# Six convolution taps on ScalarE and the DMA engines, two block sums by DMA, and one store on another queue

## The chip, the cores and the metric

The kernel runs on one core of a Trainium2 chip. A core has five instruction streams that run beside each other and wait for each other by semaphores: TensorE (PE in the profile; PEld is its weight load), VectorE (DVE), ScalarE (ACT), GpSimd (POOL) and SyncE (SP), which here only issues transfers. Transfers are issued from the queues of SP, ACT and POOL and carried out by 16 DMA engines that the queues share. A transfer issued from POOL can add what it reads to what stands at its target ("accumulating transfer" below). The metric is the device time of one execution in microseconds, the median of the runs.

## The reference

One block of a streaming encoder, for a sequence of 512 with 1024 channels, in float32:

```python
h = h + 0.5 * _swiglu(_rmsnorm(h, ffn1_norm), ffn1_w_in, ffn1_w_out)      # D_FF = 2816
z = _rmsnorm(h, mix_norm) @ w_in
conv_a, conv_gt, q, k, v, r, g_lr = split(z)                              # 512, 512, 256, 256, 512, 512, 16
y_conv = _conv_module(conv_a, conv_gt, conv_w, conv_b, conv_ln_g, conv_ln_b)
y_gla  = _gla(q, k, v, r, g_lr, gate_w_up, gate_b, gla_norm)              # 4 heads, chunks of 64
h = h + concatenate([y_conv, y_gla]) @ w_out
h = h + 0.5 * _swiglu(_rmsnorm(h, ffn2_norm), ffn2_w_in, ffn2_w_out)
h = h + sigmoid(_rmsnorm(h, ple_norm) @ ple_w_gate) * (p @ ple_w_proj)
out = _rmsnorm(h, final_norm)

def _conv_module(a, b, w_dw, b_dw, ln_g, ln_b):
    glu = a * sigmoid(b)
    y = causal_depthwise_conv(glu, w_dw, width=31) + b_dw                 # 512 channels, each with its own 31 taps
    return silu(_layernorm(y, ln_g, ln_b))                                # mean and variance over the 512 channels
```

The case is about the convolution (31 taps for each channel) and the LayerNorm behind it, whose mean needs the sum over all 512 channels.

## The kernel before, in words

Channels lie on the 128 partitions and time along a row, so most tiles are 128x512 in float32 (256 KB). Matrix products are made in three matmuls of a reduced-precision type: each weight is split into a high part (`wh`, a cast by ScalarE) and a low part (`wl` = weight - high part). The low part is either a DVE subtraction (`low`) or, with `added`, two steps: ScalarE writes the negated high part to `wl`, and a transfer on GpSimd's queue adds the raw weight to it.

The stages follow one another: the first FFN to about 337 us, the mixer to about 520 us, the second FFN to about 845 us, then the gate of the per-layer input, the last norm and the stores. In the mixer come the input projections (blocks of output channels, `zblock`, then blocks of time, `tokblock`), the chunks of the linear attention, and the output projection, whose first half over the attention channels (`first_part`) runs before the convolution's channels are ready.

The convolution has four blocks of 128 channels, c = 0 to 3, with the sums in `acc[c]` (`cv` in the trace) and the inputs in `glu[c]` (`glr`, `glu`, `glu` and `en` in the trace's rows of taps, since buffers are named by their first tenant). `conv_steps(c)` (line 1013) is a generator: the first step writes the last tap with the bias, the next 30 steps add one tap each, all on DVE. Tap w is late by 30 - w columns, so that the first tap (w = 0) covers 482 columns and the last of them (w = 29) 511. `taps(n)` (line 1025) takes n steps, in turn from the two oldest convolutions that are not done; calls of it stand between the other DVE work of the mixer. What is left of the last one is run through behind `first_part(1, ...)` (line 1456).

For the LayerNorm's mean the four blocks are added to `acc012` (`r` in the trace): two DVE additions at lines 1424 and 1439, between taps, and `acc[3]` at line 1460 behind the last tap. PE multiplies it with the constant matrix `mean`, inside `first_part(5, ...)` at its step 6; DVE then subtracts the mean from each `acc[c]`, ScalarE squares, DVE adds the squares.

The order of PE, DVE and ScalarE is that in which the code is written: the helper class `Ordered` (line 46, which is why nearly all rows of the trace name L46) ties each instruction behind the one before it on its engine. The transfers on SP and GpSimd are ordered by the scheduler of the tile framework. A transfer waits on its issuing queue until its data and its target are ready, and all later ones on that queue wait behind it.

At the prediction's places the names are: `wl<-wr` on POOL, low parts of weights by `added` (wk[1] of the key projection, wo[2] of the output projection); `sm<-wr`, the low part of an early piece of the per-layer input's product; `wa<-wr` x4, the low parts of wo[4] and wo[5] in four tiles of 256 KB; `wr<-in_w_out` and `wr<-in_ffn_w_in` on SP, loads of raw weights. The last four stores of the tail are made by `first_half`, `scaled_out` and `second_half` (lines 1815 to 1831), with the calls from line 1942.

Of the kernel before, what the change touches and what calls it, by code (L numbers as in the profile page):

```python
# [11 lines left out]
AF = mybir.ActivationFunctionType  # L12
ALU = mybir.AluOpType
PSUM = bass.MemoryType.PSUM

P = 128
SEQ = 512
# [4 lines left out]
WIDTH = 31  # L22
PAD = WIDTH - 1
# [39 lines left out]
def block_kernel(ctx: ExitStack, tc: tile.TileContext, a: dict, out: bass.AP):  # L63
    nc = tc.nc
    pe, dve, act, pool = (Ordered(tc, e) for e in (nc.tensor, nc.vector, nc.scalar, nc.gpsimd))
# [15 lines left out]
    def nm(s):  # L81
        uid[0] += 1
        return f"{s}_{uid[0]}"
# [6 lines left out]
    def bt2(dt=F32R, s="a"):  # L90
        t = big.tile([P, 2, SEQ], dt, tag="A", bufs=NA, name=nm(s))
        hi, lo = t[:, 0], t[:, 1]
        whole_of[id(hi)] = hi, t
        return hi, lo

    def bt(dt=F32, s="a"):
        if dt not in other:
            t, other[dt] = bt2(dt, s)
            return t
        return other.pop(dt)  # L100

    def cvt(dt=F32, s="cv"):
        return big.tile([P, SEQ], dt, tag="CV", bufs=NCV, name=nm(s))

    def tmp(s, w=SEQ, dt=F32, bufs=2):
        return tp.tile([P, w], dt, tag=s, bufs=bufs, name=nm(s))
# [65 lines left out]
    cw = col[:, ncol - DC:]  # L172
# [5 lines left out]
    def vec(name, c, n=1):  # L178
        at = first_of[name] + c
        return col0[:, at:at + n] if at < DC else col[:, at - DC:at - DC + n]  # L180
# [42 lines left out]
    def high(r3):  # L223

        nk, nc_ = r3.shape[1], r3.shape[2]
        hi = wp.tile([P, 1024], F32R, tag="wh", bufs=6, name=nm("wh"))
        lo = wp.tile([P, 1024], F32R, tag="wl", bufs=6, name=nm("wl"))
        h3 = hi[:, :nk * nc_].rearrange("p (k c) -> p k c", k=nk)
        l3 = lo[:, :nk * nc_].rearrange("p (k c) -> p k c", k=nk)
        act.copy(h3, r3)  # L230
        return h3, l3, r3
# [6 lines left out]
    def added(w):  # L238

        h3, l3, r3 = w  # L240
        act.mul(l3, r3, -1.0)
        pool.dma_start(out=l3.bitcast(F32), in_=r3, accum_op=ALU.add)
        return w
# [766 lines left out]

    glu, acc, conv = [], [cvt() for _ in range(4)], []

    def conv_steps(c):
        y, g, tap = acc[c], glu[c], cw[:, c * WIDTH:(c + 1) * WIDTH]
        dve.tensor_scalar(y, g, tap[:, PAD:WIDTH], vec("conv_b", c), ALU.mult, ALU.add)
        yield
        for w in range(PAD):
            late = PAD - w
            dve.scalar_tensor_tensor(out=y[:, late:], in0=g[:, 0:SEQ - late], scalar=tap[:, w:w + 1],
                                     in1=y[:, late:], op0=ALU.mult, op1=ALU.add)  # L1020
            yield

    turn = [0]

    def taps(n):

        for _ in range(n):
            if not conv:
                return
            i = turn[0] % min(2, len(conv))  # L1030
            turn[0] += 1
            try:
                next(conv[i])
            except StopIteration:
                conv.pop(i)
# [8 lines left out]
    def glu_value(ps):  # L1044
        a1 = tmp("u1")
        dve.tensor_tensor(out=a1, in0=ps, in1=rsb, op=ALU.mult)
        return a1

    def glu_out(a1, sg):
        g = bt(s="glu")  # L1050
        dve.tensor_tensor(out=g, in0=a1, in1=sg, op=ALU.mult)
        glu.append(g)
        conv.append(conv_steps(len(glu) - 1))
# [50 lines left out]

    taps(1)
    wq.append(added(high(raw_q[1])))


    pb = zblock(w2b[0], hg)
# [44 lines left out]
    wk.append(added(high(raw_k[1])))  # L1154
    taps(5)
    glu_out(glu_value(pa), sg)


    qdec, qneg, kneg, kpos, kdec = [], [], [], [], []
# [49 lines left out]
    def tokblock(w, t, mid={}):  # L1209

        ps = bank()
        ts = slice(t * P, (t + 1) * P)
        i = 0
        for k in range(DC):
            wh, wl = w[k // 2][:2]
            xh, xl = hg[k]
            for x, y in ((xh, wh), (xl, wh), (xh, wl)):
                if i in mid:
                    mid[i]()
                pe.matmul(ps, x[:, ts], y[:, k % 2, :], start=(i == 0), stop=(i == 3 * DC - 1))  # L1220
                i += 1
        return ps
# [31 lines left out]
    def chunk_sums(cs):  # L1254
        for j in range(2):
            if len(kvs) == j:
                kvs.append([bank(), bank()])
            for c in cs:
                s0 = (c % 2) * CH
                for i in range(2):  # L1260
                    h = 2 * j + i
                    pe.matmul(kvs[j][c % 2][i * HK:(i + 1) * HK, (c // 2) * HV:(c // 2 + 1) * HV],
                              kdt[j][s0:s0 + CH, (c // 2) * P + i * HK:(c // 2) * P + (i + 1) * HK],
                              vt[c // 2][s0:s0 + CH, h * HV:(h + 1) * HV], start=True, stop=True)
# [18 lines left out]
    def out_of(t, h):  # L1283
        c = 2 * (t % 2) + h // 2
        return ops[2 * (t // 2) + h % 2][:, c * HV:(c + 1) * HV]
# [21 lines left out]
    def chain(cs):  # L1307
        for c in cs:
            for j in range(2):
                state(j, c)  # L1310
# [39 lines left out]
    def early_parts():  # L1350
        hi, lo = (kept_p[:, i * 2 * P:(i + 1) * 2 * P].rearrange("p (k c) -> p k c", k=2) for i in range(2))
        act.copy(hi, early_p)
        added((hi, lo, early_p))
        early_x[:] = [(hi[:, k], lo[:, k]) for k in range(2)]
        wh, wl = (wp.tile([P, 1024], F32R, tag="sm", bufs=2, name=nm("sm")).rearrange("p (k c) -> p k c", k=2)
                  for _ in range(2))
        act.copy(wh, early_w)
        early_wh[:] = added((wh, wl, early_w))[:2]
# [3 lines left out]
    def oload(n):  # L1362
        for i in range(n, n + 2):
            raw_o[i] = load(a["w_out"], 0, DC, i * P, P)

    def ohigh(n):
        return (high4 if n in (4, 5) else high)(raw_o[n])
# [21 lines left out]
    for t in range(TB):  # L1389
        if t == 0:  # L1390
            ps = tokblock(wr, t, {5: lambda: chunk_sums(range(7))})
            chain(range(7))
            taps(3)
            oload(4)
        elif t == 1:
            ps = tokblock(wr, t, {2: outputs})
            early_parts()
            taps(15)
            by_t = "p (t h) -> p t h"
            so3 = so.rearrange(by_t, h=4)  # L1400
            dve.tensor_tensor(out=so3, in0=so3, in1=rs2.unsqueeze(2).to_broadcast([P, TB, 4]), op=ALU.mult)
            rso = rsqrt_mean(so, HV * HK, 16, between=lambda: taps(5))
            rso3 = rso.rearrange(by_t, h=4)
            dve.scalar_tensor_tensor(out=rso3, in0=rso3, scalar=HK ** -0.5,
                                     in1=rs.unsqueeze(2).to_broadcast([P, TB, 4]), op0=ALU.mult, op1=ALU.mult)
        else:
            ps = tokblock(wr, t)
        r = bt(s="r")
        act.activation(r, ps, AF.Silu, scale=rs[:, t:t + 1])
        rt.append(r)  # L1410
        if t == 1:
            oload(2)
            for n in (4, 5):
                wo[n] = [added(w) for w in ohigh(n)]
            ytok = []
            for i in range(TB):
                y = bt(s="y")
                for h in range(4):
                    vs = slice(h * HV, (h + 1) * HV)
                    act.activation(y[:, vs], out_of(i, h), AF.Copy, scale=rso[:, 4 * i + h:4 * i + h + 1])  # L1420
                ytok.append(y)
        if t == 3:
            acc012 = bt(s="acc012")
            dve.tensor_tensor(out=acc012, in0=acc[0], in1=acc[1], op=ALU.add)
        if t > 0:
            taps((0, 2, 5, 1)[t])
            for i in {1: (0,), 2: (1, 2), 3: (3,)}[t]:
                dve.tensor_tensor(out=ytok[i], in0=ytok[i], in1=rt[i], op=ALU.mult)
# [7 lines left out]
            pe.transpose(yps[h][:, t * P:(t + 1) * P], ytok[t][:, h * HV:(h + 1) * HV], ident)  # L1436
    pe.matmul(pq, early_x[0][0], early_wh[1][:, 0, :], start=False, stop=False)
    projected(pq, 0, early_wh, early_x, (1,))
    dve.tensor_tensor(out=acc012, in0=acc012, in1=acc[2], op=ALU.add)
    taps(1)  # L1440
    for h in range(4):
        mix[4 + h] = gsplit(yps[h], vec("gla_norm", h), "yg")
# [89 lines left out]
    for k in range(4):  # L1532
        for n in range(3):
            w, ps = half[n]
# [199 lines left out]
    hf, hl = {}, {}  # L1734
# [77 lines left out]
        dve.scalar_tensor_tensor(out=q, in0=r, scalar=nh, in1=r, op0=ALU.mult, op1=ALU.mult)  # L1812
        dve.scalar_tensor_tensor(out=q, in0=q, scalar=1.5, in1=r, op0=ALU.add, op1=ALU.mult)

    def scaled_out(t, e, src, *queue):
        y = bt(s="y")
        act.activation(y, src, AF.Copy, scale=roots[t][2])
        put(t, e, y, *queue)

    def put(t, e, y, queue=nc.sync):  # L1820
        queue.dma_start(out=out[0, t * P:(t + 1) * P, e * SEQ:(e + 1) * SEQ], in_=y)

    def first_half(t, e):
        y = bt(s="y")
# [3 lines left out]
    def second_half(t, e):  # L1828
        y = bt(s="y")
        dve.scalar_tensor_tensor(out=y, in0=hl[t], scalar=roots[t][2], in1=gfin[e], op0=ALU.mult, op1=ALU.mult)  # L1830
        put(t, e, y)
# [110 lines left out]
    first_half(0, 0)  # L1942
    scaled_out(0, 1, gained)
    newton(1)
    scaled_out(1, 0, hf[1], act)
    second_half(1, 1)


# [48 lines left out]
```

## Time and profile before

| | |
|---|---|
| time, median of 3 runs (lowest, highest) | 921.93 us (921.61, 922.09) |
| profiled execution, its own time | 921.48 us |
| its span, first to last instruction | 919.7 us |
| mean granted TensorE clock | 0.998 |
| PE busy | 910.7 us (99%) |
| DVE busy | 816.7 us (89%) |
| ACT busy | 511.7 us (56%) |
| POOL busy | 60.3 us (7%) |
| mean DMA rate | 129 GB/s |

The page gives shares of one profiled execution. A share is a mean over all stages: DVE is 89% busy over the whole span and 19.45 of 20 us from 460 to 480 us. A row of a timeline has the start in us, the duration in us, the engine, line, operation, target<-sources, and in brackets the engine's idle time before it with what ended it; x18 means that 18 instructions in a row were put together, with the time from the first start to the last end. Rows with a q behind the engine are issues of transfers; how long these take to land stands in the DMA view (number, KB each, median us from issue to landing).

### The profile page before, as it was taken

What the parts mean: (1) busy time and instruction counts of PE and PEld (TensorE: products, weight loads), DVE (VectorE), ACT (ScalarE), POOL (GpSimd) and SP (SyncE); (2) the same over time, 40 slices, a digit from 0 to 9 for tenths busy, and PEclk for the clock granted to TensorE, in tenths of its full rate; (3) what the DMA queues carried; (4) which work ended last, traced back from release to release, by engine and by line L of the source; (5) the groups of instructions that cost most, each with busy time, mean ns of one, the idle gap of its engine ahead of it and who ended that gap; (6) DMA issues with size and microseconds to landing.
All of it is one profiled execution on the core that took longest, in us unless ns stands there. A gap on an engine that the chain in (4) does not pass through costs nothing.

```text
span 919.7 us, 12838 instructions
## 1 busy us (share of the span) xinstructions
PE 910.7 (99%) x4948; PEld 779.7 (85%) x4948; DVE 816.7 (89%) x1090; ACT 511.7 (56%) x746; POOL 60.3 (7%) x76
## 2 busy tenths in 40 slices
PE   9999999999999999999999999999999999999996
PEld 8899888888888887788887889888888888888885
DVE  6699989999989766999996779899999999997896
ACT  7755354445454574463665875455445444556884
POOL 0120000000000111001130020000000000000121
PEclk9999999999999999999999999999999999999999
DMA  9534333224334692245572563333223322358454
GB/s 350 186 100 136 117 112 122 91 73 135 115 92 115 158 295 51 69 118 158 139 166 93 137 157 97 115 116 126 87 84 130 122 89 87 118 155 240 92 99 131
DMA packets 37149, 118.89 MB, mean 129 GB/s; under 512 B 4192, under 2 KB 4960, under 8 KB 37088
## 3 DMA queue, kind: packets, MB, share of 16 engines
q1 hardware_dynamic: 30176, 97.22, 31.8%
q0 software_dynamic: 6624, 20.58, 12.5%
q8 instruction: 39, 0.64, 0.3%
q10 hardware_dynamic: 288, 0.27, 0.1%
q14 instruction: 22, 0.18, 0.1%
HBM read 96.43 MB, written 2.10 MB: 107 GB/s over the span
## 4 chain that ended last, share of the span: by engine, by line
PE 96%; DVE 2%; ACT 1%; issue 0%; POOLq 0%
PE ps L46 56%; PE pd L46 40%; DVE cv L46 1%; ACT wa L46 0%; ACT sq L46 0%; DVE yg L46 0%; DVE r L46 0%; DVE y L46 0%; ACT r L46 0%; ACT sm L46 0%; ACT px L46 0%; POOLq L1993 0%; ACT s L46 0%; DVE u L46 0%; DVE g L46 0%
## 5 line engine op out<-in xcount | busy, mean ns | idle before, releaser
L46 DVE TENSOR_TENSOR wl<-wr,wh 128x1024 fp32r<-128x1024 f32 (+2 forms) x159 | 185.9, 1179 | 16.9 <-ACT wh L46 16.4
L46 ACT CAST wh<-wr 128x1024 fp32r<-128x1024 f32 (+2 forms) x177 | 175.4, 1023 | 14.4 <-PE ps L46 7.7
L46 PE MATMUL pd<-hg,wh 128*128 128x512 f32 x576 | 150.0, 391 | 0.0
L46 PE MATMUL ps<-act,wh 128*128 128x512 f32 x448 | 137.9, 389 | 0.0
L46 PEld LDWEIGHTS pd<-hg,wh 128*128 128x128 f32 x576 | 105.9, 188 | 21.1 <-DVE u L46 0.4
L46 PE MATMUL ps<-hg,wh 128*128 128x512 f32 (+1 forms) x448 | 117.0, 345 | 0.0
L46 PEld LDWEIGHTS ps<-act,wh 128*128 128x128 f32 x448 | 84.1, 188 | 17.5
L46 ACT ACTIVATE s<-g 128x512 f32<-128x512 f32 x48 | 30.4, 632 | 117.6 <-DVE g L46 117.6
L46 PE MATMUL pd<-t,wh 128*128 128x512 f32 x392 | 95.3, 391 | 0.0
L46 ACT COPY sq<-pd 128x1024 f32<-128x1024 f32 x45 | 45.8, 1017 | 86.7 <-PE pd L46 52.3
L46 PE MATMUL ps<-act,wl 128*128 128x512 f32 x224 | 87.1, 389 | 0.0
L46 PEld LDWEIGHTS ps<-hg,wh 128*128 128x128 f32 x448 | 78.0, 190 | 10.5 <-issue 0.5
L46 PEld LDWEIGHTS pd<-t,wh 128*128 128x128 f32 x392 | 71.4, 189 | 13.4
L46 PE MATMUL pd<-hg,wl 128*128 128x256 f32 (+1 forms) x544 | 81.5, 289 | 0.0
L46 PEld LDWEIGHTS pd<-hg,wl 128*128 128x128 f32 x544 | 73.9, 191 | 5.1
L46 PE MATMUL ps<-hg,wl 128*128 128x512 f32 (+1 forms) x224 | 77.0, 344 | 0.0
L46 ACT CAST wh<-sm 128x1024 fp32r<-128x1024 f32 x42 | 44.0, 1050 | 55.6 <-DVE sm L46 50.1
L46 DVE TENSOR_TENSOR wl<-sm,wh 128x1024 fp32r<-128x1024 f32 x42 | 51.0, 1219 | 5.1 <-ACT wh L46 5.1
L46 DVE TENSOR_TENSOR sq<-pd,sq 128x1024 f32<-128x1024 f32 x45 | 54.8, 1218 | 0.4 <-PE pd L46 0.4
L46 PE MATMUL ps<-wh,hg 128*128 128x512 f32 x176 | 54.4, 390 | 0.0
L46 PE MATMUL pd<-t,wl 128*128 128x256 f32 x392 | 52.4, 283 | 0.0
L46 PEld LDWEIGHTS pd<-t,wl 128*128 128x128 f32 x392 | 50.6, 191 | 1.5
(300 smaller groups left out, 1625.2 us busy)
## 6 DMA issues: line engine op xcount, KB each, us to landing
wr<-in_ffn_w_in SPq DMA_DIRECT2D x84, 512.0 KB, 3.6
wr<-in_ffn_w_out SPq DMA_DIRECT2D x32, 512.0 KB, 3.6
wl<-wr POOLq DMA_DIRECT2D x20, 512.0 KB, 5.4
wr<-in_ffn_w_out SPq DMA_DIRECT2D x16, 384.0 KB, 3.3
wr<-in_w_blocks SPq DMA_DIRECT2D x12, 512.0 KB, 5.7
wr<-in_w_rows SPq DMA_DIRECT2D x8, 512.0 KB, 3.8
wr<-in_w_out SPq DMA_DIRECT2D x8, 512.0 KB, 5.9
wq<-in_ple_w_gate SPq DMA_DIRECT2D x8, 512.0 KB, 4.3
```

The source lines that it names most:

```text
L46: inst = call(*args, **kwargs)
```

## The change

It has three parts.

1. The first two taps (w = 0 and 1) of blocks 0, 1 and 2 leave DVE. A new function `taps_apart(c, t, u)` lets ScalarE multiply the shifted input by the tap, once into t and once into u, and issues on GpSimd's queue an accumulating transfer u += t (482 columns). Behind the last DVE tap of these blocks `conv_steps` issues another, acc[c] += u (483 columns). Block 0's two multiplications are written behind the high part of wq[1], those of blocks 1 and 2 behind the high part of wk[1].
2. acc012 is made by transfers: a plain copy of acc[0] on SP's queue, acc[1] added by an accumulating transfer, acc[2] by another. DVE still adds acc[3].
3. The last store but one, which was issued from ScalarE's queue, is issued from SP's, as all others.

```diff
@@ -1010,14 +1010,27 @@
+    apart = {}
+
+    def taps_apart(c, t, u):
+
+        g, tap = glu[c], cw[:, c * WIDTH:(c + 1) * WIDTH]
+        for w, y in ((0, t), (1, u)):
+            late = PAD - w
+            act.activation(y[:, late:], g[:, 0:SEQ - late], AF.Copy, scale=tap[:, w:w + 1])
+        pool.dma_start(out=u[:, PAD:], in_=t[:, PAD:], accum_op=ALU.add)
+        apart[c] = u
+
     def conv_steps(c):
...
-        for w in range(PAD):
+        for w in range(0 if c == 3 else 2, PAD):
             late = PAD - w
             dve.scalar_tensor_tensor(out=y[:, late:], in0=g[:, 0:SEQ - late], scalar=tap[:, w:w + 1],
                                      in1=y[:, late:], op0=ALU.mult, op1=ALU.add)
+            if w == PAD - 1 and c < 3:
+                pool.dma_start(out=y[:, PAD - 1:], in_=apart[c][:, PAD - 1:], accum_op=ALU.add)
             yield
@@ -1104,6 +1117,7 @@
     wq.append(added(high(raw_q[1])))
+    taps_apart(0, bt(s="ta"), bt(s="ta"))
@@ -1154,6 +1168,8 @@
     wk.append(added(high(raw_k[1])))
     taps(5)
     glu_out(glu_value(pa), sg)
+    for c, s_ in ((1, "g1"), (2, "u1")):
+        taps_apart(c, tmp(s_), tmp(s_))
@@ -1419,9 +1435,10 @@
-        if t == 3:
+        if t == 1:
             acc012 = bt(s="acc012")
-            dve.tensor_tensor(out=acc012, in0=acc[0], in1=acc[1], op=ALU.add)
+            nc.sync.dma_start(out=acc012, in_=acc[0])
+            pool.dma_start(out=acc012, in_=acc[1], accum_op=ALU.add)
@@ -1436,7 +1453,7 @@
-    dve.tensor_tensor(out=acc012, in0=acc012, in1=acc[2], op=ALU.add)
+    pool.dma_start(out=acc012, in_=acc[2], accum_op=ALU.add)
@@ -1812,13 +1829,13 @@
-    def put(t, e, y, queue=nc.sync):
-        queue.dma_start(out=out[0, t * P:(t + 1) * P, e * SEQ:(e + 1) * SEQ], in_=y)
+    def put(t, e, y):
+        nc.sync.dma_start(out=out[0, t * P:(t + 1) * P, e * SEQ:(e + 1) * SEQ], in_=y)
@@ -1942,7 +1959,7 @@
-    scaled_out(1, 0, hf[1], act)
+    scaled_out(1, 0, hf[1])
     second_half(1, 1)
```

The order of the matmuls on PE is the same. On the other engines rows move at three places. In the order, acc012 is the tile y_4322, and cv_3193 to cv_3196 are acc[0] to acc[3].

GpSimd's queue near the end of the output projection's first half, before:

```order
L46 DMA sm_4234<-wr_4036 128x1024
L46 DMA wa_4277<-wr_4132 128x512
L46 DMA wa_4279<-wr_4132 128x512
L46 DMA wa_4285<-wr_4134 128x512
L46 DMA wa_4287<-wr_4134 128x512
L46 DMA wl_4419<-wr_4273 128x1024
```

and in the changed kernel:

```order
L46 DMA sm_4250<-wr_4052 128x1024
L46 DMA cv_3195<-u_633_3613 128x483
L46 DMA wa_4293<-wr_4148 128x512
L46 DMA wa_4295<-wr_4148 128x512
L46 DMA wa_4301<-wr_4150 128x512
L46 DMA wa_4303<-wr_4150 128x512
L46 DMA y_4322<-cv_3194 128x512
L46 DMA y_4322<-cv_3195 128x512
L46 DMA wl_4437<-wr_4289 128x1024
```

acc[2]'s two taps are added ahead of the four wa, and the two sums of acc012 stand between the wa and the low part of wo[2]. The first of the two waits until the copy of acc[0] has landed, the second until the first has.

SP's queue at the same time, before:

```order
L216 DMA wr_4426<-in_w_out 128x1024
L216 DMA wr_4428<-in_w_out 128x1024
L216 DMA wr_4467<-in_ffn_w_in 128x1024
L216 DMA wr_4469<-in_ffn_w_in 128x1024
```

and in the changed kernel:

```order
L216 DMA wr_4444<-in_w_out 128x1024
L216 DMA wr_4446<-in_w_out 128x1024
L1440 DMA y_4322<-cv_3193 128x512
L216 DMA wr_4479<-in_ffn_w_in 128x1024
L216 DMA wr_4481<-in_ffn_w_in 128x1024
```

The copy of acc[0] stands behind the last load of w_out, although acc[0] itself is done some 60 us earlier; that load waits for sm to land.

DVE near the end of block 0 (cv_3193), before:

```order
L46 SCALAR_TENSOR_TENSOR cv_3193<-glr_3354,col,cv_3193 128x510
L46 SCALAR_TENSOR_TENSOR cv_3194<-glu_3403,col,cv_3194 128x500
L46 TENSOR_TENSOR ed_3640<-ps_3603,en_3559 128x512
L46 TENSOR_TENSOR q_3682<-ps_3603,cum_3550 128x512
L46 SCALAR_TENSOR_TENSOR cv_3193<-glr_3354,col,cv_3193 128x511
```

and in the changed kernel:

```order
L46 SCALAR_TENSOR_TENSOR cv_3193<-glr_3354,col,cv_3193 128x510
L46 COPY decay_3663<-cum_3554 128x8
L46 SCALAR_TENSOR_TENSOR cv_3194<-glu_3403,col,cv_3194 128x500
L46 SCALAR_TENSOR_TENSOR cv_3193<-glr_3354,col,cv_3193 128x511
L46 SCALAR_TENSOR_TENSOR cv_3194<-glu_3403,col,cv_3194 128x501
L46 TENSOR_SCALAR cv_3195<-glu_3516,col 128x512
L46 TENSOR_TENSOR ed_3654<-ps_3617,en_3563 128x512
```

Block 0's last tap (511 columns) now stands ahead of the two multiplications ed and q. Behind that tap the transfer acc[0] += u is issued on GpSimd's queue (`cv_3193<-ta_3411` there), and the low part of wk[1] behind that.

More of the change, by code (lines that the diff above doesn't have):

```diff
@@ L1813, in newton, with scaled_out @@
         dve.scalar_tensor_tensor(out=q, in0=q, scalar=1.5, in1=r, op0=ALU.add, op1=ALU.mult)
-    def scaled_out(t, e, src, *queue):
+    def scaled_out(t, e, src):
         y = bt(s="y")
         act.activation(y, src, AF.Copy, scale=roots[t][2])
-        put(t, e, y, *queue)
-    def put(t, e, y, queue=nc.sync):
-        queue.dma_start(out=out[0, t * P:(t + 1) * P, e * SEQ:(e + 1) * SEQ], in_=y)
+        put(t, e, y)
+    def put(t, e, y):
+        nc.sync.dma_start(out=out[0, t * P:(t + 1) * P, e * SEQ:(e + 1) * SEQ], in_=y)
     def first_half(t, e):
```

## The prediction

> **What bounds the kernel now.** I read the page first: busy times, then the chain that ended last.
>
> ```profile
> PE 910.7 (99%) x4948; PEld 779.7 (85%) x4948; DVE 816.7 (89%) x1090; ACT 511.7 (56%) x746; POOL 60.3 (7%) x76
> ...
> PE 96%; DVE 2%; ACT 1%; issue 0%; POOLq 0%
> ```
>
> TensorE (PE) is busy 910.7 of 919.7 us, and the chain stays on it for 96%. So I asked next for everything that PE waits for; the whole answer is two rows:
>
> ```profile
> PE ps L46 <- PEq L1987: 0.8, 1, 0.8
> PE ps L46 <- DVE r L46: 0.3, 1, 0.3
> ```
>
> 0.8 us is PE's sequencer once, 0.3 us DVE's r at one matmul. VectorE (DVE) is nearly full in the mixer, but its time sets nothing except those 0.3 us: relieving it elsewhere is worth nothing, because PE is not waiting for it. The matmul with the 0.3 us is the one the change works on. PE's timeline there, and DVE's:
>
> ```profile
> 479.18 4.24 PE L46 MATMUL ps<-yg,wa 128*128 128x512 f32 x18
> 483.72 1.12 PE L46 MATMUL ps<-r,mean 128*128 128x512 f32 x2 [0.30 <-DVE r L46]
> ...
> 486.30 0.39 PE L46 MATMUL ps<-yg,wl 128*128 128x512 f32 x1
> ```
>
> ```profile
> 470.85 0.68 DVE L46 TENSOR_TENSOR r<-cv,cv 128x512 f32<-128x512 f32 x1
> ...
> 472.05 0.68 DVE L46 TENSOR_TENSOR r<-r,cv 128x512 f32<-128x512 f32 x1
> 472.65 0.73 DVE L46 SCALAR_TENSOR_TENSOR cv<-en,col,cv 128x502 f32<-128x502 f32 x1
> ...
> 475.94 6.99 DVE L46 SCALAR_TENSOR_TENSOR cv<-en,col,cv 128x503 f32<-128x503 f32 x9
> 482.97 0.69 DVE L46 TENSOR_TENSOR r<-r,cv 128x512 f32<-128x512 f32 x1
> ```
>
> r is acc012, the sum of the convolution's blocks: acc[0]+acc[1] at 470.85, acc[2] at 472.05, acc[3] at 482.97. PE reads it in the `mean` matmul at 483.72; without the wait PE would be there at 483.72 - 0.30 = 483.42. Whatever delivers acc012 later than now stops PE, in its order, with everything behind it. This is the place that decides.
>
> **The change, part by part.**
>
> *Six taps leave DVE.* Nine taps take 6.99 us, 0.78 each, in the drain. Six taps and two sums make some 6 x 0.73 + 2 x 0.68 = 5.7 us less for DVE, spread over 370 to 483 us. Three of the nine taps of the drain are left, so DVE would have acc[3] ready at about 478, not 483. That is worth 0.3 us at most, the only wait on DVE, and only if acc012's other terms are there too.
>
> *ScalarE takes six multiplications.* Nearest row: 48 ACTIVATEs of 128x512 of 632 ns each (first row below, a group of the page). Two stand behind the cast of wq[1], four behind that of wk[1], some 1.3 and 2.5 us, ahead of these waits in ScalarE's timeline:
>
> ```profile
> L46 ACT ACTIVATE s<-g 128x512 f32<-128x512 f32 x48 | 30.4, 632 | 117.6 <-DVE g L46 117.6
> ...
> 379.85 0.63 ACT L46 ACTIVATE s<-g 128x512 f32<-128x512 f32 x1 [11.58 <-DVE g L46]
> ...
> 415.56 1.05 ACT L46 CAST wh<-wr 128x1024 fp32r<-128x1024 f32 x1 [3.05 <-PE ps L46]
> ```
>
> 1.3 lies in 11.58, 2.5 in 3.05. Cost 0; without that cover the casts of weights that follow would come 2.5 us late.
>
> *Six accumulating transfers on GpSimd's queue for the taps.* They are issued in order with the low parts of the weights. Most precede nothing urgent. The tight place is behind `cv_3193<-ta` (acc[0] += its two taps): it waits for conv 0's last DVE tap, and the low part of wk[1] is queued behind it.
>
> ```profile
> 403.43 0.87 POOL L46 DMA_DIRECT2D wl<-wr  x1 [12.65 <-ACT wl L46]
> ...
> wl<-wr POOLq DMA_DIRECT2D x1, 512.0 KB, 5.2
> ...
> 407.32 0.74 DVE L46 SCALAR_TENSOR_TENSOR cv<-glr,col,cv 128x511 f32<-128x511 f32 x1
> ...
> 410.55 0.39 PE L46 MATMUL ps<-hg,wl 128*128 128x512 f32 x1
> ```
>
> (issue on GpSimd's queue, KB and us to landing, last tap on DVE, PE's use.)
>
> Now it lands at 403.43 + 5.2 = 408.6, 1.9 us before PE uses it. Conv 0's last tap ended at 408.1; in DVE's new order two taps of conv 0, two of conv 1 and the two multiplications `ed` and `q` no longer stand ahead of it, 6 x 0.65 = 3.9 us (0.65 from one tap's start to the next), so it ends near 404.2. Then comes the issue (0.87), and 247 KB of the accumulate ahead of the weights. That makes wk[1]'s low part 1.6 to 2.4 us later: a PE stall of 0 to 0.5 us. I take 0.1.
>
> *acc012 by three transfers.* Before, two DVE sums. Now a plain copy of acc[0] on SyncE's (SP's) queue, then acc[1] by an accumulating transfer, then acc[2] by another, each issued only when the one before it has landed. The copy stands on SP behind the last loads of w_out, the accumulates on GpSimd behind sm, the new `acc[2] += u1` and the four wa. When do these go? GpSimd's and SP's issues in the timeline, then what the DMA view says of the issues from 464 to 470 us:
>
> ```profile
> 463.44 0.91 POOL L46 DMA_DIRECT2D sm<-wr  x1
> 464.05 3.86 POOL L46 DMA_DIRECT2D wa<-wr  x4
> 477.65 0.86 POOL L46 DMA_DIRECT2D wl<-wr  x1 [9.74 <-ACT wl L46]
> ```
>
> ```profile
> 442.10 26.50 SPq L216 DMA_DIRECT2D wr<-in_w_out  x5
> 471.25 13.91 SPq L216 DMA_DIRECT2D wr<-in_ffn_w_in  x4
> ```
>
> ```profile
> wa<-wr POOLq DMA_DIRECT2D x4, 256.0 KB, 7.3
> sm<-wr POOLq DMA_DIRECT2D x1, 512.0 KB, 4.8
> wr<-in_w_out SPq DMA_DIRECT2D x1, 512.0 KB, 8.0
> ```
>
> sm lands at 463.44 + 4.8 = 468.2; SP's last w_out load, which waits for that, is issued there and takes 8.0 us, to 476.3. Why so long? The queues' packets, MB and share from 469 to 473 us, and from 473 to 476.5:
>
> ```profile
> q0 software_dynamic: 349, 0.62, 109.1%
> q1 hardware_dynamic: 1, 0.00, 0.3%
> ...
> q1 hardware_dynamic: 252, 0.96, 69.6%
> q0 software_dynamic: 105, 0.18, 31.7%
> ```
>
> While GpSimd's backlog of accumulates (q0) was moving, SP's load (q1) got one packet in 4 us. [...] In the changed kernel the copy of acc[0] is issued right behind that load, about 468.7, and the backlog is longer: `acc[2] += u1` is 247 KB, at 0.62 MB in 4 us (155 KB/us) 1.6 us; part of it moves beside the load, as in the second pair of rows, so I take 1.2. The w_out load lands at 477.5, and the copy's 256 KB behind it, at q1's 0.96 MB in 3.5 us (274 KB/us, while shared), 0.8 us later: 478.3. Bounds: 477.0 (the load no later than now) and 479.5 (1.6, and 0.8 for the ffn load beside it).
>
> The price of one accumulate of 256 KB, from the transfers of other sizes and from the twelve wa of 256 KB:
>
> ```profile
> px<-u POOLq DMA_DIRECT2D x1, 128.0 KB, 2.7
> ...
> wl<-wr POOLq DMA_DIRECT2D x1, 512.0 KB, 4.9
> ...
> DMA to landing us min/median/max: 3.9/5.5/10.4
> ```
>
> A third of the way in size from 2.7 (128 KB) to 4.8 (sm) or 4.9 (512 KB) lies 2.7 + 2.1/3 = 3.4 us; the fastest wa took 3.9, in company. Bounds: 3.3 from below, 4.7 from above (half way from the fastest to the median 5.5, in which several queue). For acc[1] I take 3.7, since SP's next loads run beside it; for acc[2] 3.4, since those loads are then held by later waits. With 0.1 for each step of semaphore and issue: 478.3 + 3.7 = 482.0, + 0.1 + 3.4 = 485.5, + 0.1 and DVE's sum 0.69 = 486.3. The mean matmul starts at 486.3 in place of 483.72: **+2.6 us**. By the bounds: 477.0 + 2 x 3.3 + 0.9 = 484.5 (+0.8), and 479.5 + 2 x 4.7 + 0.9 = 489.8 (+6.1; both ends at once are unlikely, +5 is my bound).
>
> [...]
>
> *What waits behind it.* The low part of wo[2] is next on GpSimd's queue (477.65 before, 4.9 us). Issued behind acc[2]'s accumulate (482.1 + 0.9) it lands at about 488. PE first uses it at 486.30 before, now 2.6 later, 488.9: just hidden, 0 to 0.5 us if not; 0. DVE's subtractions, squares and the column sums shift with the matmul; nothing catches up, PE being full afterwards: the 2.6 us goes to the end.
>
> *The last stores.*
>
> ```profile
> 915.23 0.72 ACT L46 ACTIVATE y<-cv,rs 128x512 f32<-128x512 f32 x1 [1.50 <-DVE rs L46]
> ...
> 915.98 0.38 ACTq L46 DMA_DIRECT2D out<-y  x1
> 916.01 0.33 SPq L1821 DMA_DIRECT2D out<-y  x1
> ...
> out<-y ACTq DMA_DIRECT2D x1, 256.0 KB, 2.8
> ...
> DMA to landing us min/median/max: 2.1/2.3/2.8
> ```
>
> (The last row is of all eight stores of `out`.)
> Now both are issued at once on two queues; the last lands at 915.98 + 2.8 = 918.8. On one queue the second is issued 0.42 later (0.33 plus the gap), 916.4, and at 2.1 to 2.6 us lands at 918.5 to 919.0: -0.3 to +0.2, I take 0. If the engines were shared badly, +0.4.
>
> **Sum**: 0 (DVE) + 0 (ScalarE) + 0.1 (wk[1]) + 2.6 (mean) + 0 (wo[2]) + 0 (store) = +2.7 us. The profiled execution took 921.48 (its span 919.7 and 1.8 around it), so 924.2; it lies 0.45 under the median of the runs, 921.93, so 924.6 there.
>
> **Rivals.**
>
> *A. The transfers are hidden.* The copy gets through early, before the backlog, and acc[2]'s accumulate lands by 482.6, so that DVE's sum is done by 483.4. Then the 0.3 us go too: 921.6, with the store 921.3 to 921.9. It needs the copy to land by about 475.4 (482.6 - 2 x 3.5 - 0.2). Against it stands the one packet in 4 us.
>
> [...]
>
> *B. The accumulates are dear.* Each takes 4.7 us or more, as among loads: 478.3 + 9.4 + 0.9 = 488.6, +4.9, and wo[2]'s low part late by 0.5: 921.93 + 5.4 = 927.3. For it: the median 5.5 of wa. Against: few other transfers then.
>
> *C. wk[1] decides.* If the last tap of conv 0 is not earlier, `acc[0] += t` is issued at 408.1, and wk[1]'s low part lands at 409 + 5.2 + 1.3 = 415.5, against 410.55: a stall of 5 us, on top of or instead of the mean's: 927 to 929. Against: two taps gone and the others moved up; it decides from a tap's end later than about 404.5.
>
> *D. DVE's time is worth something*: PE's rows leave room for 0.3 us and the tail for 0.3, so 921.3 at best; it needs A.
>
> **How the numbers follow.** A measurement of this kernel tells about 0.2%, 1.84 us, from no change. Forecast (+1.9 to +4, one wait of 2 to 4 us) 0.5; A and D 0.15; a shortened wait, between A and forecast (+0.3 to +1.8) 0.14; B 0.1; C 0.08; a faster kernel by over 0.2% only if something unseen gives 1.8 us, 0.03. Slower is 0.5 + 0.1 + 0.08 = 0.68; same is 0.15 + 0.14 = 0.29; faster 0.03. The range leaves out C, half of B, and the lower edge of A: 921.4 to 927.0. The forecast's own range is 923.8 to 926.
>
> **What would show it.** PE's wait at the mean matmul, named as DVE's or a transfer's, about 2.9 us in place of 0.3, with DVE idle from about 478 until acc[2]'s accumulate has landed at about 485.4. The copy of acc[0] should land 9 us or so after its issue. wk[1]: a wait of PE at a low part near 410 us, under 0.5. The last store lands 2.1 to 2.6 us after an issue 0.4 us behind the other. If PE shows no wait at the mean, the forecast falls; if DVE ends its taps at 478 and the accumulates have landed before 482, A is right; if the wait is there but the time isn't longer, PE was not what sets the end.

## The result and the profile after

| kernel | time, median (lowest, highest) | ratio to before, 95% interval |
|---|---|---|
| before | 922.01 us (921.61, 922.18) | |
| changed | 929.42 us (928.97, 930.09) | 1.0082 [1.0069, 1.0095] |

The change makes the kernel 7.4 us slower, where 2.7 us were forecast, and the time lies outside the range (921.4 to 927.0). The profiled execution took 929.95 us with a span of 928.2. Its page begins as before: PE at 99%, the rest less than PE. PE is busy 3.9 us longer than before although it runs the same 4948 matmuls.

```profile
PE 914.6 (99%) x4948; PEld 781.8 (84%) x4948; DVE 811.7 (87%) x1082; ACT 515.5 (56%) x752; POOL 67.1 (7%) x84
...
PEclk9999999999999999999998999999999999999999
```

One slice of the clock row has an 8, where before all had 9. What PE waits for:

```profile
PE ps L46 <- DVE y L46: 4.5, 2, 4.2
PE ps L46 <- PEq L2004: 0.8, 1, 0.8
PE ps L46 <- DMA wl<-wr: 0.2, 1, 0.2
```

4.2 us in one piece on DVE's y, which is now acc012, where it was 0.3 us; 0.3 us on another y; 0.2 us on wk[1]'s low part. PE's timeline at the long wait:

```profile
481.03 4.24 PE L46 MATMUL ps<-yg,wa 128*128 128x512 f32 x18
489.44 2.08 PE L46 MATMUL ps<-y,mean 128*128 128x512 f32 x2 [4.17 <-DVE y L46]
490.53 3.55 PE L46 MATMUL ps<-yg,wa 128*128 128x512 f32 x6
```

Before, the same two `mean` matmuls took 1.12 us and the six behind them 1.95. Now it is 2.08 and 3.55. The clock by stretches (stretch, its length, PE's busy time and matmuls, granted clock, DMA share, GB/s):

```profile
483.00:486.00 3.00, 2.27 (x11) 1.00 0.43 80
486.00:489.00 3.00, 0.00 (x0) 0.82 0.84 152
489.00:490.00 1.00, 0.56 (x1) 0.50 1.06 201
...
493.00:494.00 1.00, 1.00 (x4) 0.50 0.66 193
494.00:495.00 1.00, 1.00 (x5) 0.63 0.71 266
495.00:496.00 1.00, 1.00 (x6) 1.00 0.29 119
```

While PE stood still, from 485.27 to 489.44 us, its granted clock went to half (0.50, from 487.92 on), and it stayed there for some 5 us after PE had gone on (to 494.74). This is the part of the loss that the waits do not list, and that the prediction does not have.

Matching the matmuls of the two profiled executions one by one (they are the same, in the same order) tells where the 8.5 us between these two executions come from: 0.8 us in the first 6 us, before the change acts; 0.4 us at wk[1]'s first low part; 0.6 us at the transposes near 472 us; 3.9 us at the mean matmul; 2.5 us in the ten matmuls behind it; 0.25 us behind PE's last matmul. The first 0.8 us is chance (below), so 7.7 us are left, against 7.4 between the medians.

Why acc012 was late: GpSimd's issues (the two `y<-cv` are acc[1] and acc[2]), SP's (the copy), and the landings of the copy and of the two in turn:

```profile
465.54 4.24 POOL L46 DMA_DIRECT2D wa<-wr  x4
480.49 0.86 POOL L46 DMA_DIRECT2D y<-cv  x1 [10.72 <-DMA y<-cv]
485.23 0.86 POOL L46 DMA_DIRECT2D y<-cv  x1 [3.88 <-DMA y<-cv]
```

```profile
469.65 1.39 SPq L1440 DMA_DIRECT2D y<-cv  x1
```

```profile
y<-cv SPq DMA_DIRECT2D x1, 256.0 KB, 10.3
...
y<-cv POOLq DMA_DIRECT2D x1, 256.0 KB, 4.5
...
y<-cv POOLq DMA_DIRECT2D x1, 256.0 KB, 3.4
```

469.65 + 10.3 = 480.0, then 480.49 + 4.5 = 485.0, then 485.23 + 3.4 = 488.6. DVE had stood ready since 480.1:

```profile
477.79 2.31 DVE L46 SCALAR_TENSOR_TENSOR cv<-en,col,cv 128x509 f32<-128x509 f32 x3
488.70 0.69 DVE L46 TENSOR_TENSOR y<-y,cv 128x512 f32<-128x512 f32 x1 [8.59 <-DMA y<-cv]
```

The two smaller places: PE's first use of wk[1]'s low part, and the transposes, in PE's timeline:

```profile
411.73 0.50 PE L46 MATMUL ps<-hg,wl 128*128 128x512 f32 x1 [0.17 <-DMA wl<-wr]
...
472.20 1.26 PE L46 MATMUL ps<-ident,y 128*128 128x128 f32 x8 [0.28 <-DVE y L46]
```

### The profile page after: what moved, and what is told of

Same layout as the page of the kernel before. It is cut to its first block, busy times and chain, and to the rows that moved or that the text cites. A ratio compares the mean times of both kernels' runs of the same rounds, so it can differ in the third digit from the quotient of the medians.

```text
span 928.2 us, 12860 instructions
## 1 busy us (share of the span) xinstructions
PE 914.6 (99%) x4948; PEld 781.8 (84%) x4948; DVE 811.7 (87%) x1082; ACT 515.5 (56%) x752; POOL 67.1 (7%) x84
## 4 chain that ended last, share of the span: by engine, by line
PE 90%; DMA 3%; issue 2%; DVE 2%; ACT 2%; POOL 0%; POOLq 0%; SPq 0%; DVEq 0%; ACTq 0%
PE ps L46 51%; PE pd L46 40%; DMA y<-cv 1%; DVE cv L46 1%; DMA wl<-wr 1%; DMA sm<-wr 1%; ACT ab L46 1%; ACT sq L46 0%; ACT L46 0%; DVE g L46 0%; ACT wa L46 0%; DVE y L46 0%; ACT sm L46 0%; DVE u L46 0%; ACT wl L46 0%
```

## The experiments

Theory 1: the loss is the late acc012, once as PE's stand (the time for which PE stands still at the mean matmul) and a second time as the half clock that the stand brings about. Against it stand, first, that the six taps cost it (traffic, ScalarE, DVE's new order), and second, that the matmuls behind the stand are slow for another reason, so that no clock is needed.

### Each part alone

**e1: the two sums of acc012 back on DVE**, taps and store as changed.

```diff
-        if t == 1:
-            nc.sync.dma_start(out=acc012, in_=acc[0])
-            pool.dma_start(out=acc012, in_=acc[1], accum_op=ALU.add)
+        if t == 3:
+            dve.tensor_tensor(out=acc012, in0=acc[0], in1=acc[1], op=ALU.add)
...
-    pool.dma_start(out=acc012, in_=acc[2], accum_op=ALU.add)
+    dve.tensor_tensor(out=acc012, in0=acc012, in1=acc[2], op=ALU.add)
```

> The changed kernel with its two sums of acc012 back on DVE (taps on ScalarE and by transfers, and the store on SP's queue, stay). Theory 1: the time went into the late acc012 (PE stands 4.2 us at the mean matmul) and into the half clock behind that stand; then this kernel is 0.2 to 1.0 us above before (922.2 to 923.0), PE has no wait over 0.5 us at the mean matmul and the granted clock stays at 1.00 there. Rival: the six taps themselves cost it, by traffic and the order of DVE; then it stays 5 to 8 us above before.

922.84 us, 1.0009 [1.0000, 1.0018]: +0.8 us of the 7.4. The mean matmul does not wait at all; the transposes do, twice:

```profile
472.58 1.26 PE L46 MATMUL ps<-ident,y 128*128 128x128 f32 x8 [0.27 <-DVE y L46]
475.04 0.66 PE L46 MATMUL ps<-ident,y 128*128 128x128 f32 x4 [0.73 <-DVE y L46]
486.11 1.02 PE L46 MATMUL ps<-r,mean 128*128 128x512 f32 x2
```

**e2: the sums by transfers alone**, on the kernel before (the same lines the other way round).

> The kernel before with the sums of acc012 by transfers alone (all taps on DVE, store as before). Here the copy of acc[0] stands one ffn load further back on SP's queue. Theory 1: acc012 is late again, PE stands 3 to 5 us at the mean matmul, the clock falls to 0.5 behind it, and the time is 5 to 8 us above before. If the stand is there and under 3 us without a fall of the clock: 2 to 3 us above. Rival (the taps cost it): within 1 us of before.

928.73 us, 1.0073 [1.0056, 1.0089]: +6.7 us, nearly the whole loss, with no tap moved. PE stood 4.7 us at the mean matmul:

```profile
488.19 2.07 PE L46 MATMUL ps<-y,mean 128*128 128x512 f32 x2 [4.66 <-DVE y L46]
489.28 3.55 PE L46 MATMUL ps<-yg,wa 128*128 128x512 f32 x6
```

The matmuls behind the stand are as slow as in the changed kernel. The first rival falls: taps and store together cost 0.8 us, the sums the rest.

**e3: the store alone**, on the kernel before.

```diff
-    scaled_out(1, 0, hf[1], act)
+    scaled_out(1, 0, hf[1])
```

> The kernel before with the last but one store on SP's queue alone. Theory 1 and the prediction's term for it: -0.3 to +0.2 us, no difference that can be measured; the last store is issued about 0.4 us behind the other and lands 2.1 to 2.6 us later. Rival: one queue serves the two one after the other, +0.4 to +0.7 us.

921.89 us, 0.9998 [0.9988, 1.0007]: no difference, as the prediction's term had it.

**e4: the copy of acc[0] and the accumulate of acc[1] written ahead of w_out's loads**, in the changed kernel.

```diff
+    acc012 = bt(s="acc012")
+    nc.sync.dma_start(out=acc012, in_=acc[0])
+    pool.dma_start(out=acc012, in_=acc[1], accum_op=ALU.add)
     oload(0)
...
-        if t == 1:
-            acc012 = bt(s="acc012")
-            nc.sync.dma_start(out=acc012, in_=acc[0])
-            pool.dma_start(out=acc012, in_=acc[1], accum_op=ALU.add)
```

> The changed kernel with the copy of acc[0] and the accumulate of acc[1] written ahead of the loads of w_out, so that only acc[2]'s accumulate is left for the end, between the wa on GpSimd's queue. Theory 1 (acc012 was late because the copy stood behind w_out's load and GpSimd's backlog): the chain of transfers is done before DVE's last tap, PE waits under 1 us at the mean matmul, the clock stays at 1.00, and the time is 0.2 to 1.5 us above before. Rival (any sum by transfers is too slow here, or the taps cost it): 5 to 8 us above.

922.84 us, 1.0009 [1.0000, 1.0018], the same as e1. acc012 (now in a buffer named pq) is copied at 430.23, and only acc[2]'s accumulate is left for the end, 5.9 us from its issue at 470.97:

```profile
430.23 0.82 SPq L1404 DMA_DIRECT2D pq<-cv  x1
```

```profile
470.97 0.87 POOL L46 DMA_DIRECT2D pq<-cv  x1 [2.98 <-DMA cv<-u]
```

DVE's last sum starts at 480.50 in place of 488.70, and PE does not wait for it. So sums by transfers are not too slow as such; what cost 6.6 us was three of them one behind the other, begun at 469.65 behind a load and GpSimd's backlog.

### What a stand of PE costs

To measure the disputed cost by itself, with no transfer changed: in the kernel before, n more DVE steps ahead of the last sum. Each writes the larger of acc[3] and acc[3] into acc[3], which changes nothing but the time.

```diff
+    for _ in range(n):
+        dve.tensor_tensor(out=acc[3], in0=acc[3], in1=acc[3], op=ALU.max)
     dve.tensor_tensor(out=acc012, in0=acc012, in1=acc[3], op=ALU.add)
```

n = 2, 3, 4 and 5 are s2 to s5.

> The kernel before, with two more DVE steps ahead of the sum acc012 += acc[3]; each writes the larger of acc[3] and acc[3], which is acc[3], into it, so nothing else changes. Each is about 0.75 us, so PE stands 1.8 us at the mean matmul in place of 0.3. Theory 1 (a stand costs its own length, and a second time by the clock only where it lasts beyond the point at which the clock falls; 2.4 and 2.6 us after PE stopped in the two runs in which it fell): the clock stays at 1.00, +1.5 us. Rival (matmuls are slower behind any stand here, by what lies in the buffers or by traffic): more than +2.5.

> The same with three more steps: PE stands about 2.6 us. Theory 1: on the edge; +2.2 without a fall of the clock, +4.5 to +5 with one, and executions of both kinds may occur. Rival without a clock: +2.2.

> The same with four more steps: PE stands about 3.3 us. Theory 1: the clock falls in many executions; +3.0 without, +5 to +5.6 with it. Rival without a clock (the stand alone): +3.0.

> The same with five more steps: PE stands about 4.1 us, as in the changed kernel, with no transfer changed. Theory 1: the clock falls to 0.5 some 2.5 us into the stand and comes back about 6.7 us later; +3.8 for the stand and +2.3 to +2.7 for the clock, +6 to +6.5 in all. Rival (the 2.5 us behind the stand in the changed kernel came from its transfers): +3.8.

PE's rows at the mean matmul, of s2, s3, s4 and s5:

```profile
485.12 1.12 PE L46 MATMUL ps<-r,mean 128*128 128x512 f32 x2 [1.77 <-DVE r L46]
```

```profile
486.40 1.57 PE L46 MATMUL ps<-r,mean 128*128 128x512 f32 x2 [2.51 <-DVE r L46]
```

```profile
487.04 2.08 PE L46 MATMUL ps<-r,mean 128*128 128x512 f32 x2 [3.24 <-DVE r L46]
```

```profile
488.26 2.08 PE L46 MATMUL ps<-r,mean 128*128 128x512 f32 x2 [3.93 <-DVE r L46]
```

| | stand of PE, above the 0.3 of before | time above before | beyond the stand | ratio |
|---|---|---|---|---|
| s2 | 1.5 us | +1.9 us (923.90) | 0.4 | 1.0022 [1.0013, 1.0031] |
| s3 | 2.2 us | +3.8 us (925.84) | 1.6 | 1.0039 [1.0026, 1.0051] |
| s4 | 2.9 us | +5.0 us (927.07) | 2.1 | 1.0051 [1.0036, 1.0066] |
| s5 | 3.6 us | +5.2 us (927.24) | 1.6 | 1.0056 [1.0041, 1.0071] |

The stand is that of the profiled execution, the time is the median of all, and the executions of one kernel differ by 1.4 us and more (s4: 925.56 to 927.56), so the third column is rough. In s2 the matmuls behind the stand are as fast as before (1.12), and the clock stays at 1.00. From s3 on they are slower, and the windows of the trace show the clock at 0.50 for 3.4 us; for s3:

```profile
486.00:487.00 1.00, 0.60 (x3) 0.97 0.02 8
487.00:488.00 1.00, 1.00 (x3) 0.50 0.00 0
...
490.00:491.00 1.00, 1.00 (x5) 0.82 0.17 66
491.00:492.00 1.00, 1.00 (x6) 1.00 0.00 0
```

There is no DMA traffic to speak of in these rows (8 GB/s, 0), so the slow matmuls are not its doing. In s3 the six executions were not all alike: five took 925.8 to 926.4 us with a mean granted clock of 0.996 or 0.997, one 923.85 with 0.998, which is about what the stand alone would give. In s4 one of four took 925.56, with 0.998 where the others had 0.995 and 0.996; it may have kept its clock too. In s2 one of ten took 926.06 where the others took 923.1 to 924.5; its clock was 0.998 and no trace of it is kept, so what it lost is open. I had expected s3 on the edge, and 2.3 to 2.7 us for the clock in s5: the edge is right, the price of the clock here is 1.6 us, because the half clock lasted 3.41 us (half of it is 1.7) and not 6.83 as in the changed kernel.

**e5: the stand filled.** In the changed kernel three more matmuls of acc[0] with the constant matrix go ahead of the true one, into the same place, and are overwritten by it.

```diff
+        for _ in range(3):
+            pe.matmul(mub, mean, acc[0], start=True, stop=True)
         pe.matmul(mub, mean, acc012, start=True, stop=True)
```

> The changed kernel with three more matmuls of acc[0] with the constant matrix ahead of the true one, into the same place, where the true one overwrites them. They take 1.06 us each, 3.2 us of the 4.2 us in which PE stood, so acc012 is as late as before. Theory 1 (2.5 us of the 7.4 are the half clock that the stand brings about): PE's wait falls to about 1 us, the clock stays at 1.00, and the time falls by 2.0 to 2.7 us against the changed kernel, to 926.7 to 927.4, although PE does more. Rival (the time is lost to the late acc012 alone): as the changed kernel, 929 to 930.

927.41 us, 1.0062 [1.0048, 1.0075]: 2.0 us less than the changed kernel, with acc012 as late as there and PE doing more. The true matmul takes 1.13 us (2.08 in the changed kernel) and the six behind it 1.95 (3.55), so no half clock shows:

```profile
484.87 2.74 PE L46 MATMUL ps<-cv,mean 128*128 128x512 f32 x6
489.19 1.13 PE L46 MATMUL ps<-y,mean 128*128 128x512 f32 x2 [1.58 <-DVE y L46]
489.75 1.95 PE L46 MATMUL ps<-yg,wa 128*128 128x512 f32 x6
```

The extra matmuls took 2.7 us, less than I had reckoned (3.2), so 1.6 us of wait were left, under the length at which s2 kept its clock. The second rival falls: the price behind the stand goes when PE is kept at work.

### What held the copy

**e6: the copy of acc[0] from ScalarE's queue**, in the changed kernel.

```diff
-            nc.sync.dma_start(out=acc012, in_=acc[0])
+            act.dma_start(out=acc012, in_=acc[0])
```

> The changed kernel with the copy of acc[0] issued from ScalarE's queue in place of SP's, at its place in ScalarE's order, about 469.8 us, with nothing ahead of it on that queue. It tells what held the copy (10.3 us on SP's queue). If it was w_out's load ahead of it on SP's queue, the copy lands 3 us or more earlier and the stand of PE falls under 2 us (924 to 926). If it was GpSimd's backlog of accumulates, which the DMA engines serve first, the copy still lands 7 us or more after its issue, at 477 or later, and the time stays within 2 us of the changed kernel (927.5 to 930).

924.34 us, 1.0027 [1.0016, 1.0038]: 5.1 us of the 7.4 are gone. ScalarE's issue, and the landing in the DMA view:

```profile
466.36 0.52 ACTq L46 DMA_DIRECT2D y<-cv  x1
```

```profile
wr<-in_w_out SPq DMA_DIRECT2D x1, 512.0 KB, 8.8
y<-cv ACTq DMA_DIRECT2D x1, 256.0 KB, 6.2
```

It landed at 472.6 in place of 480.0. 3.3 us of this is the earlier issue (I had reckoned with 469.8; ScalarE's order has it at 466.36), 4.1 us the shorter way. The bytes by queue from 469 to 473 us show the copy (q10) moving beside GpSimd's backlog (q0), the transfers that were already issued there and had not landed:

```profile
q0 software_dynamic: 285, 0.52, 89.8%
q10 hardware_dynamic: 144, 0.26, 19.2%
```

In the changed kernel SP's queue (q1) moved nothing at all from 468 to 474 us; then came the load's bytes, and the copy's from 476.6 on. So the copy's place behind the load of w_out held it, and the load itself began 4.7 us after its issue. The backlog did not keep the copy from moving in e6, but its first bytes came 3.3 us after the issue there too, and as the issue was also earlier, the run doesn't divide the 4.1 us between the two. The accumulates then met the backlog themselves: acc[1]'s, issued at 473.07, took until 480.98, when acc[2]'s was issued. PE stood 1.26 us, and the mean matmul behind it took 1.13 us, the six after that 1.95, so no half clock shows.

### What the taps cost, and whether anything beats the kernel before

**e7: e1 with two taps in place of five ahead of the products that the transposes wait for.**

```diff
-            taps((0, 2, 5, 1)[t])
+            taps((0, 2, 2, 1)[t])
```

> The kernel of e1 (six taps apart, sums of acc012 on DVE) with two taps in place of five ahead of the products that PE's transposes wait for near 472 us; the other three move into the end of the last convolution. e1 lost 0.8 us; PE's waits on DVE's y there were 1.0 us, as five taps of one block in a row take 0.77 us each where two blocks in turn take 0.65. Theory: that wait goes, the time falls by 0.6 to 1.0 us to within 0.4 us of before (921.8 to 922.4), the wait of 0.2 us on wk[1]'s low part staying. Rival (the 0.8 us is traffic or ScalarE): 922.6 to 923.0.

921.34 us, 0.9996 [0.9987, 1.0005]. The waits at the transposes are gone and so is the one at the mean matmul (0.3 us in the kernel before); that on wk[1] stays:

```profile
PE ps L46 <- PEq L2003: 0.8, 1, 0.8
PE ps L46 <- DMA wl<-wr: 0.2, 1, 0.2
```

This is 1.5 us under e1, more than the 0.6 to 1.0 expected. Against the kernel before it is 0.6 us lower by the medians, which the interval does not tell from no difference. The five taps in a row, in e1 and in the kernel before:

```profile
468.06 3.86 DVE L46 SCALAR_TENSOR_TENSOR cv<-en,col,cv 128x502 f32<-128x502 f32 x5
```

```profile
467.68 0.73 DVE L46 SCALAR_TENSOR_TENSOR cv<-en,col,cv 128x500 f32<-128x500 f32 x1
468.33 0.74 DVE L46 SCALAR_TENSOR_TENSOR cv<-glu,col,cv 128x511 f32<-128x511 f32 x1
468.99 0.73 DVE L46 SCALAR_TENSOR_TENSOR cv<-en,col,cv 128x501 f32<-128x501 f32 x1
```

Before, taps of two blocks stood in turn, one each 0.65 us. With two taps fewer, block 2 is done earlier, and the five taps are all of block 3, each adding to what the one before has just written: 3.86 / 5 = 0.77 us. The four steps from tap to tap are 0.12 us longer each, which is the 0.5 us by which the first product comes late in e1. The other wait of e1, 0.73 us, has another source: one call of `taps` ahead of the last product wrote nothing before, as it met the end of block 2, and now writes a tap (at 473.64, 0.66 us). e7 takes 2.3 us of taps from ahead of the products, more than either, so the two are told apart by the trace and not by a run.

**f1: what the runs point to.** Blocks 1 and 2 alone give up their first two taps, the copy and acc[1]'s accumulate stand early as in e4, three taps in place of five, store on SP's queue.

```diff
-    taps_apart(0, bt(s="ta"), bt(s="ta"))
...
-            taps((0, 2, 5, 1)[t])
+            taps((0, 2, 3, 1)[t])
```

> What the runs so far point to: blocks 1 and 2 alone give their first two taps to ScalarE and transfers (no wait on wk[1]), copy of acc[0] and accumulate of acc[1] ahead of w_out's loads, three taps in place of five ahead of the transposes, store on SP's queue. All known waits of PE but the start's should be gone. Theory: -0.6 to +0.2 us against before, so at best 921.4: there was never more than 0.3 us of DVE's time on PE's path. Rival (the mixer is bound by DVE and the four taps and two sums are worth their time): 2 us or more faster.

922.33 us, 1.0004 [0.9995, 1.0013]: not faster, and 0.1 us above the expected band. wk[1]'s wait is gone; a wait of 0.8 us at the mean matmul has come. DVE is not what is late: its last seven taps end at 481.76, and it then waits 2.1 us for a transfer, acc[2]'s accumulate into acc012 (here `pq`). PE's row, DVE's, and GpSimd's issues:

```profile
484.63 1.12 PE L46 MATMUL ps<-pq,mean 128*128 128x512 f32 x2 [0.81 <-DVE pq L46]
...
476.32 5.44 DVE L46 SCALAR_TENSOR_TENSOR cv<-en,col,cv 128x505 f32<-128x505 f32 x7
483.88 0.69 DVE L46 TENSOR_TENSOR pq<-pq,cv 128x512 f32<-128x512 f32 x1 [2.12 <-DMA pq<-cv]
...
467.04 2.60 POOL L46 DMA_DIRECT2D cv<-u  x1
480.49 0.87 POOL L46 DMA_DIRECT2D pq<-cv  x1 [10.85 <-DMA cv<-u]
```

With all 31 taps of block 0 on DVE, block 2's last tap ends at 466.4 in place of 462.9 in the changed kernel. Its accumulate `cv<-u` thus stands behind the four wa and lands at 480.1, 13 us after its issue, and only then does the next one go. It is the chain of the changed kernel again, with two links.

No kernel tried here is faster than the one before by more than its measurement tells.

## Why the prediction was wrong

**What bounds the kernel** was right, as far as the runs go. PE's wait of 0.3 us and the tail's 0.3 were all that the prediction saw to gain, and the 0.6 us of the best version (e7) is not told from nothing.

**The place** was right: the time is lost at the mean matmul, by the three transfers in a chain, with DVE done (480.1) 8.6 us before its last sum. e1 and e2 show it from both sides.

**The size of the stand** was too small: 2.9 us forecast, 4.17 measured. The terms: the copy landed at 480.0, not 478.3 (issued 0.95 us later than put, and 10.3 us on its way in place of 9.6); acc[1]'s accumulate was issued 0.5 us behind that, not 0.1, and took 4.5 us, not 3.7; acc[2]'s took 3.4, as put. PE itself came to the matmul at 485.27, not 483.42, so 1.85 us later than in the profile before (0.8 us of it chance), which took as much off the stand again. The copy's term failed on its reading too: the row with one packet of q1 in 4 us was taken to say that GpSimd's backlog holds back what is issued behind it. In e6 a hardware queue moved beside the backlog (0.26 MB on q10 and 0.52 on q0 from 469 to 473 us); what the copy had ahead of it was w_out's load on its own queue, and that load's late start. Why these transfers began 3.3 (e6's copy) and 4.7 us (w_out's load in the changed kernel) after their issue during the backlog is open; in the kernel before, w_out's load was issued at 468.27 and got its first bytes at 473.

**The step that failed** is the sentence that the stand's 2.6 us "goes to the end", one to one. It priced the stand and put the matmuls behind it at nothing. With this stand of 4.17 us PE's clock went to 0.50 for 6.83 us, 2.5 us more here. The stand of 2.9 us that was forecast would most likely have brought some 1.6 to 2 us more, an estimate from s3 (1.6 beyond a stand of 2.5 us) and s4 (2.1 beyond 3.2). In the two profiled executions the mean matmul comes 3.9 us later where 2.6 were forecast, the clock adds 2.5 where nothing was, and the transposes 0.6 where nothing was. Without the clock the changed kernel would have taken some 926.9 us, an estimate from 929.42 - 2.5, which lies just inside the range. None of the rivals had the clock; B had a longer stand, at the same price per us. A stand of 2.5 us was enough for a half clock of 3.41 us (s3).

**wk[1]** cost 0.4 us, 0.2 of it listed as a wait, inside the 0 to 0.5 forecast and above the 0.1 taken. **ScalarE's six multiplications** cost nothing that shows. **The store** was right at 0 (e3). **wo[2]'s low part** was hidden, as forecast.

**DVE's six taps** were priced at 0, as time that nobody waits for. They cost 0.6 us at the transposes: which taps stand in a row had changed (0.77 us each in e1, 0.65 before). The diff of DVE's order showed this; only its place near wk[1] was read.

**The rivals.** A (hidden) is what e4 makes of it: it needs the chain ahead of the loads. C's 927 to 929 came nearest in number, and by luck: its stall of 5 us at wk[1] did not occur. B's chain came out in part: acc[1]'s accumulate took 4.5 us, near its 4.7, acc[2]'s 3.4. D is right in that no version gained more than 0.6 us (e7), and that not beyond what a measurement tells.

## What to carry to other kernels

A wait that PE takes on was not linear here: waits of 1.3, 1.6 and 1.8 us (e6, e5, s2) left the clock alone, and waits of 2.5 to 4.7 us (s3, s4, s5, the changed kernel, e2) cost 1.6 to 2.5 us more for it in nearly every execution. Nothing was measured between 1.8 and 2.5. So a forecast of a wait near 3 us in this kernel should be made with that step in it, and in another kernel the step is worth a run like s2 to s5. The sum of three terms by transfers had three latencies in a row (10.3 + 4.5 + 3.4 us): start such a sum where its terms are ready, not where the sum is needed, and look at what stands ahead of each link on its own queue (a load on SP's here, the four wa on GpSimd's in f1). Work taken off an engine that nobody waits for can still cost (0.6 us at the transposes here), when it changes which of its instructions follow each other.

## What the runs showed that I had not expected

**How long the half clock lasted.** The trace's clock records, in us of the span: half clock from, full clock again from.

```
           half      full     length of the half clock
after    487.92    494.74     6.83
e2       485.90    492.73     6.83
s3       486.95    490.36     3.41
s4       486.85    490.27     3.41
s5       488.07    491.48     3.41
```

The clock fell 2.4 us (e2), 2.65 (changed kernel), 3.05 (s4) and 3.7 (s5) after PE had stopped; in s3 PE had stood for 2.51 us and been back at work for 0.55 when it fell. In s3, s4 and s5 PE was at work before the fall or within 0.2 us of it, and the half clock lasted 3.41 us. In the changed kernel and in e2 PE stood for 1.5 and 2.3 us more behind the fall, and it lasted 6.83. Why the fall comes at different times in the stands, and why one execution of s3 went without the loss, no run shows.

**The first grant of the full clock moved by up to 3 us between the profiled executions**: 4.1 us (s2) to 7.0 us (e1), and 4.7 before, 6.7 in e3, where nothing differs until the last stores. The first matmuls were slower until then, 0.63 us where they later took 0.40. The profiled execution of before, with its grant at 4.7, and that of the changed kernel, with 6.6:

```profile
5.05 0.40 PE L46 MATMUL pd<-hg,wh 128*128 128x512 f32 x1
```

```profile
5.24 0.63 PE L46 MATMUL pd<-hg,wh 128*128 128x512 f32 x1
```

By its 22nd matmul e3 was 1.05 us behind the profiled execution of before. Two profiled executions of this kernel are not to be compared to better than that.

**A tap on DVE that adds to what the one before it wrote** took 0.77 to 0.78 us in these traces (five in 3.86 us in e1, nine in 6.99 before), one that alternates with another block 0.65 from start to start (467.68, 468.33, 468.99 before); all are 128x500 to 128x511 in float32.
